# Expert weights loaded as 16 KiB of one expert or as 8 KiB of each of two

## The chip, the core and the metric

The kernel runs on one core of a Trainium2 chip. It is one launch for one sequence of 256 tokens of width 1024, all in float32. The metric is the time of one execution on the device in microseconds (us). Each time below is a median of three runs or comes from one profiled execution.

## What is computed

The reference is one encoder block: three token mixers (gated linear attention, a Fourier mixer, attention into memory tokens), a gated merge, a LayerNorm, and then a sparse feed-forward layer of 32 experts, of which each token takes four. The change touches the experts alone:

```python
logits = (hf @ w_router + b_router)
top_val, top_idx = lax.top_k(logits, 4)
top_w = softmax(top_val)
# for each expert e, on the rows xb of the tokens that chose it:
gu = xb @ w_gu[e] + b_gu[e]            # w_gu[e]: [1024, 2048]
gate, up = split(gu, 2)
gate = minimum(gate, 7.0); up = clip(up, -7.0, 7.0)
act = (up + 1.0) * (gate * sigmoid(1.702 * gate))
out = act @ w_down[e] + b_down[e]      # w_down[e]: [1024, 1024]
# y[token] += weight * out, over the token's four experts; then a last LayerNorm
```

An expert has 8 MiB of gate and up weights and 4 MiB of down weights, so that all 32 have 402.7 MB.

## The kernel before

**Stages.** The mixer comes first and fills about the first quarter of the time. The function `moe` follows. The experts are taken in 16 pairs. A token's row lies in one of 64 slots of its expert, and the two experts of a pair share the tensor engine's array: expert 0 has columns 0 to 63 of it, expert 1 columns 64 to 127, and their results are the two halves of the partitions of one PSUM tile. `pair_mm` (L969) issues a matmul for expert 0 and then one for expert 1; each has 128 rows of contraction, 64 columns of tokens as its weights and 512 columns of expert weights that stream through. A float32 matmul shows as two instructions in the trace.

**A pair's work.** `up(p)` (L975) takes eight row blocks k, each 128 rows of the contraction; for each it calls `pair_mm` for four PSUM tiles (`gps`, n = 0 to 3), which makes 8 matmuls or 16 instructions for one k. `swiglu` follows on the vector and scalar engines. `gather(p + 1)` (L899) picks the next pair's token rows with 16 one-hot matmuls (`pick`, L822, 32 instructions). `weigh` (L916, with transposes at L923) and `transpose_act` (L993, L998) prepare the next products. `down(p - 1)` (L1002) takes eight row blocks again, with two PSUM tiles (`yps`): 32 matmuls or 64 instructions. `combine` (L1018, L1021) adds the pair's result to the tokens' sums. `add_bias` (L960, L966) starts every PSUM tile with the biases. The last pair's down product is `last_down` (L1034): its columns come in three parts, and each of its loads holds one expert only.

**Loads.** A pair takes 12 loads of 2 MiB: eight by `load_gu` (L765, issued at L771) and four by `load_down` (L775, issued at L778). Every load fills one slot of a ring of ten (`new_unit`, L758), 16 KiB in each partition. `load_gu` loads one row block k of both experts: 8 KiB of a row of expert 0 and 8 KiB of a row of expert 1. `load_down` loads two row blocks of both experts: 8 KiB (two rows of 4 KiB) of each. The first six loads of pair 0 stand in slots that the mixer no longer needs (`early_load`, L1219); two more of the first loads use room that is needed later (L928). All of them are issued by SyncE's queue, and a load waits there until the matmuls that read its slot before it are done.

**Order.** Within an engine the instructions run in the order of the program, and that order is fixed when the kernel is built. A planner makes it: it walks through the traced instructions with its own estimates of their times, and whenever an engine is free it takes, of the instructions that it believes ready, the one that stands first in the source. So an instruction that it believes to be waiting for a load is passed over, and later work takes its place. Only the issues of the loads (L771) and a few matmuls that keep the array busy (`spin`, L873) are held to the order of the source.

Of the kernel before, what the change touches and what calls it, by code (L numbers as in the profile page):

```python
# [18 lines left out]
D = 1024  # L19
# [34 lines left out]
class Rstd:  # L54
    """(v + eps) ** -0.5 with one Newton step, in two parts; v is [128, n]."""
# [26 lines left out]
def ln_stats(K, x):  # L82
    """Mean and variance of the rows of x: [128, D] SBUF."""
    nc, sm = K.nc, K.small
    st = sm.tile([128, 2, 6], F32, name="bst", tag="st")
    for j in range(2):
        nc.vector.bn_stats(st[:, j], x[:, j * 512:(j + 1) * 512])
    mv = sm.tile([128, 2], F32, name="bmv", tag="mv")
    nc.vector.bn_aggr(mv, st)
    return mv  # L90


def ln_apply(K, x, mv, r, g, b, out, cut=D):
    """Columns from cut on by the scalar engine and gpsimd, the rest by the vector engine."""
    nc = K.nc
    if cut < D:
        c = slice(cut, D)
        t = K.small.tile([128, 8], F32, name="nmr", tag="sm")[:, 0:1]
        nc.vector.scalar_tensor_tensor(t, mv[:, 0:1], -1.0, r, ALU.mult, ALU.mult)
        nc.scalar.activation(out[:, c], x[:, c], AF.Identity, bias=t, scale=r)  # L100
        nc.gpsimd.tensor_tensor(out[:, c], out[:, c], g[:, c], ALU.mult)
        nc.gpsimd.tensor_tensor(out[:, c], out[:, c], b[:, c], ALU.add)
    if cut:
        c = slice(0, cut)
        nc.vector.scalar_tensor_tensor(out[:, c], x[:, c], mv[:, 0:1], g[:, c], ALU.subtract, ALU.mult)
        nc.vector.scalar_tensor_tensor(out[:, c], out[:, c], r, b[:, c], ALU.mult, ALU.add)


def layer_norm(K, x, g, b, out):
    """x: [128, D] SBUF; out = (x - mean) * rstd * g + b."""  # L110
    mv = ln_stats(K, x)
    ln_apply(K, x, mv, rstd(K, mv[:, 1:2], LN_EPS, 1), g, b, out, 768)


def split(K, src, hi, lo):
    """hi = src rounded to the multiplier's width, lo = the exact rest."""
    K.nc.scalar.activation(hi, src, AF.Copy)  # L117
    K.nc.vector.tensor_tensor(lo, src, hi.bitcast(F32), ALU.subtract)  # L118


class Split:
    """[128, n, S] operand kept as two float32r parts, in tiles of four rows."""
# [8 lines left out]
def transpose_split(K, x, tau, T, j):  # L131
    """x: [128 tokens, 1024]; writes the transpose of half j into T's columns of token tile tau."""
    nc = K.nc
    ps = K.ps.tile([128, 4, 128], F32, name="tps", tag="ms")
    for c in range(4):
        nc.tensor.transpose(ps[:, c], x[:, (j * 4 + c) * 128:(j * 4 + c + 1) * 128], K.ident)
    sl = slice(tau * 128, tau * 128 + 128)
    split(K, ps, T.hi[j][:, :, sl], T.lo[j][:, :, sl])
# [10 lines left out]
def load_w(K, W, c0, n, kn, eng=None):  # L149
    """Columns c0..c0+n of a [kn * 128, ...] matrix."""  # L150
    w = K.wraw.tile([128, 2048], F32, name="wraw", tag="wraw")[:, :kn * n].rearrange("p (k n) -> p k n", k=kn)
    (eng or K.nc.sync).dma_start(w, W[:, c0:c0 + n].rearrange("(k p) n -> p k n", p=128))
    return w


def split_w(K, w):
    """Parts of a [128, m, n] piece of weights, m * n <= 1024."""
    m, n = w.shape[1:]
    parts = []
    for name in ("whi", "wlo"):  # L160
        t = K.wspl.tile([128, 1024], F32R, name=name, tag=name)[:, :m * n]
        parts.append(t.rearrange("p (m n) -> p m n", m=m))
    split(K, w, *parts)
    return parts


class Background:
    """Work for the vector engines, woven between the projections' chunks."""
# [29 lines left out]
def mixer(ctx: ExitStack, K, A):  # L198
    tc, nc = K.tc, K.nc
    pool = lambda name, bufs: ctx.enter_context(tc.tile_pool(name=name, bufs=bufs))  # L200
    # in the order in which the ring's slots follow below
# [25 lines left out]
    # ---- inputs, LayerNorm and transposes  # L227
# [20 lines left out]
    # four tiles in one, of what is done with when the GLA branch is gated  # L248
    part = K.early.tile([128, 4, D], F32, name="parts", tag="ring2")

    # four more, up to the two small branches' operands, and four up to a gate
# [14 lines left out]
    with tc.manual_schedule(engines={mybir.EngineType.DVE, mybir.EngineType.PE, mybir.EngineType.Activation}):  # L266
        # brings the array's clock up
# [33 lines left out]
    # four tiles in one: the two directions' queries and keys, before them what makes the decays  # L301
# [7 lines left out]
    def project_T(W, c0, nch, X, kn, evac, first=None):  # L309
        """Transposed products: evac(first chunk, psum [128, m, S]) for pairs of 128 columns."""  # L310
# [14 lines left out]
    def project_tok(W, c0, X, evac, last=False, eng=None):  # L325
        """512 columns by token: evac(tau, psum [128, 512])."""
# [26 lines left out]
    # ---- low-rank decay inputs  # L353
# [9 lines left out]
    # ---- memory tokens: LayerNorm and transposes  # L363
# [27 lines left out]
    # ---- decays: log-sigmoid (times 16) and its running sums  # L391
# [31 lines left out]
    # ---- q, k (transposed), v (by token)  # L423
# [11 lines left out]
    # Inside a tile of 128 tokens the decays are taken from its middle; between the two tiles from the border.  # L435
# [34 lines left out]
    # ---- values  # L470
# [19 lines left out]
    # ---- memory keys and queries  # L490
# [14 lines left out]
    # ---- attention weights into the memory tokens  # L505
# [34 lines left out]
    # ---- memory values, FNet inputs  # L540
# [6 lines left out]
    # ---- the branches' inner products  # L547
# [59 lines left out]
    def fnet_gen():  # L607
# [5 lines left out]
        # column 128 - k of the cosines is column k, of the sines minus column k: half of each is enough  # L613
# [11 lines left out]
        # row S - s of the cosines is row s, of the sines minus row s: half of each is enough  # L625
# [27 lines left out]
    # ---- output gate of the GLA branch  # L653
# [33 lines left out]
    # ---- gates, branch projections, merge  # L687
# [44 lines left out]
    # ---- output projection, residual, LayerNorm  # L732
# [25 lines left out]
def new_unit(K, shape):  # L758
    """The next ring slot, 16 KiB a partition."""
# [5 lines left out]
def load_gu(K, A, p, k, w=None):  # L765
    """One row a partition of a pair's gate and up weights."""
    if (p, k) in K.loaded:
        return K.loaded[p, k]
    w = K.loaded[p, k] = w or new_unit(K, (2, 2 * D))
    src = A["w_gu"][0, 2 * p:2 * p + 2, k // 2 * 256:k // 2 * 256 + 256].rearrange("e (p k) n -> p e k n", p=128)  # L770
    K.tc.keep_in_program_order(K.nc.sync.dma_start(w, src[:, :, k % 2]))  # L771
    return w


def load_down(K, A, p, i):  # L775
    """Two rows a partition of a pair's down weights."""
    w = new_unit(K, (2, 2, D))
    K.nc.sync.dma_start(w, A["w_down"][0, 2 * p:2 * p + 2, i // 2 * 512:i // 2 * 512 + 512].rearrange(  # L778
        "e (p k) n -> p e k n", p=128)[:, :, i % 2 * 2:i % 2 * 2 + 2])
    return w  # L780
# [11 lines left out]
def moe(ctx, K, A):  # L792
    tc, nc = K.tc, K.nc
    h1 = K.h1
    # the slots in the order in which the mixer's pools lay, numbered by when those are done with
# [10 lines left out]
    # ---- router: logits, top 4, slot of each token in its experts  # L806
# [11 lines left out]
    def pick(p, tau, P, t, j, last, first):  # L818
        """Adds a token tile's chosen rows, transposed, to half j of the pair's operand."""
# [42 lines left out]
    def place(tau):  # L862
        """slot + 1 where the expert is chosen, 0 elsewhere."""
# [9 lines left out]
    def spin(n, out=None):  # L873
        """Keeps the array's clock up while it waits."""
# [24 lines left out]
    def gather(p):  # L899
        """The pair's rows, transposed, by a one-hot product."""  # L900
# [15 lines left out]
    def weigh(p, P):  # L916
        """The way back: slots to tokens, times the tokens' weights."""
# [9 lines left out]
    # as much of the weights as there is room for, also where the activations and the sums will be  # L927
# [10 lines left out]
    # ---- softmax weights of the chosen experts, the largest count, the residual  # L938
# [21 lines left out]
    def add_bias(acc, p, at, first):  # L960
        """acc[n] (+)= the pair's biases, by rows of the table picked with a one-hot operand."""
# [7 lines left out]
    def pair_mm(acc, xT, k, w, first, last):  # L969
        """Both experts of a pair at once, each in its half of the array's columns."""  # L970
        for e in range(2):
            nc.tensor.matmul(acc[e * 64:e * 64 + 64], xT[:, k, e * 64:e * 64 + 64], w[:, e], start=first, stop=last,  # L972
                             skip_group_check=True)

    def up(p, xT):  # L975
# [4 lines left out]
        for k in range(8):  # L980
            w = load_gu(K, A, p, k)
            for n in range(4):
                pair_mm(g[n], xT, k, w[:, :, n * 512:n * 512 + 512], not early and k == 0, early and k == 7)
# [18 lines left out]
    def down(p, aT, G):  # L1002
# [3 lines left out]
        for i in range(4):  # L1006
            w = load_down(K, A, p, i)
            for k in range(2):
                for n in range(2):
                    pair_mm(yy[n], aT, i * 2 + k, w[:, :, k, n * 512:n * 512 + 512], False, i * 2 + k == 7)  # L1010
            if p == NE // 2 - 2 and i < 3:
                spin(2, mps()[:, :128])
# [14 lines left out]
    def last_parts(p):  # L1027
        """The last pair's columns, in ever smaller parts, so that little is left to do when the last of them arrives."""
# [5 lines left out]
    def last_down(p, aT, G, parts):  # L1034
# [3 lines left out]
        for sl, ps, ks in parts:  # L1038
            for k0, k1 in zip(ks, ks[1:]):
# [3 lines left out]
                for k in range(k0, k1):  # L1043
                    pair_mm(ps, aT, k, w[:, :, k - k0], False, k == 7)
# [7 lines left out]
    def norm_rows(gb):  # L1052
        """The last LayerNorm's gain and offset on every partition."""
# [30 lines left out]
def overflow(ctx, K, A):  # L1084
    """Slots 64..255 of every expert."""
# [93 lines left out]
def finish(K, A, o, st, g, b):  # L1179
    """The last LayerNorm of z, with the statistics of its quarters, into the output."""  # L1180
# [15 lines left out]
def block(tc, A):  # L1196
# [4 lines left out]
    with tc.tile_pool(name="cst", bufs=1) as c, tc.tile_pool(name="small", bufs=8) as sm, \  # L1201
# [17 lines left out]
        def early_load(e):  # L1219
            """The first pair's row e, where the mixer no longer needs the room."""  # L1220
# [46 lines left out]
```

## Time and profile before

| | us |
|---|---|
| median of 3 runs (1262.57 to 1264.88) | 1263.12 |
| the profiled execution, first to last instruction (span) | 1260.8 |
| matmuls on the tensor engine (PE), busy | 1228.3 |
| vector engine (DVE), busy | 374.8 |
| scalar engine (ACT), busy | 249.2 |

The profiled execution's span is 2.3 us below the median of the runs, which also contains what lies around the first and the last instruction. In the rows further down, PE is the tensor engine's matmul unit, PEld its weight load, SPq SyncE's queue; L972 is line 972 of the kernel. A row of the timeline joins neighbouring instructions of one kind on one engine; x16 means 16 of them. The times of matmuls in it are modelled at their ends, so that two neighbouring rows overlap by some tenths of a microsecond.

### The profile page before, as it was taken

The numbers are of one execution on the slowest core, as the hardware profiler recorded it, in microseconds if no ns is written. First come the engines' busy times: TensorE is split into PE (matmuls) and PEld (weight loads), VectorE is DVE, ScalarE is ACT, GpSimd is POOL, SyncE is SP. The second block draws the span as 40 slices with busy tenths as digits, with TensorE's granted clock in tenths as the row PEclk, the third lists the DMA queues.
The fourth block names the chain that finished last, engine by engine and source line by source line (L and its number), as shares of the span: only waits on it lengthen the run. The fifth ranks groups of instructions, "written<-read, shape, count | busy, mean of one in ns | idle before, by whom it ended". The sixth has DMA issues, their size and how long they took to land.

```text
span 1260.8 us, 15216 instructions
## 1 busy us (share of the span) xinstructions
PE 1228.3 (97%) x6601; PEld 652.0 (52%) x6601; DVE 374.8 (30%) x572; ACT 249.2 (20%) x404; POOL 60.1 (5%) x76
## 2 busy tenths in 40 slices
PE   7899999999999999999999999999999999999995
PEld 6799999999644344343333434343434334343332
DVE  6996555486311020201111111111121111111023
ACT  4655555453211010101010000101010101000010
POOL 3460000000000000000000000000000000000000
PEclk8899999999999999999999999899999999999998
DMA  8665557597899999999999999999999999999990
GB/s 285 203 213 169 201 201 234 216 336 285 354 393 409 424 427 427 427 428 428 427 427 427 427 427 427 427 427 427 427 428 428 428 427 426 428 428 427 428 359 36
DMA packets 105707, 459.31 MB, mean 364 GB/s; under 512 B 4614, under 2 KB 51264, under 8 KB 57508
## 3 DMA queue, kind: packets, MB, share of 16 engines
q1 hardware_dynamic: 105224, 457.66, 89.2%
q8 instruction: 54, 0.88, 0.3%
q10 hardware_dynamic: 284, 0.55, 0.1%
q14 instruction: 17, 0.14, 0.0%
q0 software_dynamic: 128, 0.07, 0.0%
HBM read 457.22 MB, written 1.05 MB: 363 GB/s over the span
## 4 chain that ended last, share of the span: by engine, by line
PE 88%; DVE 7%; ACT 2%; issue 1%; DMA 1%; POOL 0%; ACTq 0%; DVEq 0%; POOLq 0%
PE gps L972 34%; PE yps L972 18%; PE pj L145 6%; PE pj L146 6%; PE pj L144 6%; PE mps L822 5%; PE mps L1021 5%; PE gps L966 2%; PE mps L998 2%; PE yps L966 1%; DVE work L786 1%; DVE wlo L118 1%; DVE work L784 1%; DVE work L787 1%; DVE work L788 1%
## 5 line engine op out<-in xcount | busy, mean ns | idle before, releaser
L972 PE MATMUL gps<-wexp,xT 128*64 128x512 f32 x2048 | 448.5, 594 | 0.0
L972 PEld LDWEIGHTS gps<-wexp,xT 128*64 128x64 f32 x2048 | 143.5, 137 | 291.7 <-issue 289.8
L972 PE MATMUL yps<-wexp,work 128*64 128x512 f32 x960 | 233.7, 611 | 0.0
L972 PEld LDWEIGHTS yps<-wexp,work 128*64 128x64 f32 x960 | 69.9, 139 | 147.1 <-issue 145.3
L118 DVE TENSOR_TENSOR wlo<-wraw,whi 128x1024 fp32r<-128x1024 f32 (+2 forms) x97 | 118.4, 1228 | 63.7 <-ACT whi L117 63.5
L1025 DVE TENSOR_TENSOR sum<-sum,mps 128x512 f32<-128x512 f32 (+1 forms) x62 | 41.6, 670 | 267.3 <-PE mps L1021 267.3
L784 DVE TENSOR_SCALAR work<-gps 128x512 f32<-128x512 f32 x32 | 22.1, 692 | 320.9 <-PE gps L972 292.2
L117 ACT ACTIVATE whi<-wraw 128x1024 fp32r<-128x1024 f32 (+2 forms) x97 | 94.8, 984 | 97.2 <-PE pj L145 82.5
L144 PE MATMUL pj<-hT,whi 128*128 128x256 f32 (+1 forms) x392 | 112.6, 287 | 0.0
L146 PE MATMUL pj<-hT,wlo 128*128 128x256 f32 (+1 forms) x392 | 110.9, 283 | 0.5 <-DVE wlo L118 0.5
L145 PE MATMUL pj<-hT,whi 128*128 128x256 f32 (+1 forms) x392 | 110.9, 283 | 0.1
L785 ACT ACTIVATE work<-work 128x512 f32<-128x512 f32 x32 | 20.1, 629 | 377.4 <-DVE work L784 377.4
L822 PEld LDWEIGHTS mps<-P,h 128*128 128x128 f32 x512 | 62.5, 196 | 22.4 <-issue 21.0
L144 PEld LDWEIGHTS pj<-hT,whi 128*128 128x128 f32 (+1 forms) x392 | 73.6, 188 | 1.0 <-ACT whi L117 0.3
L146 PEld LDWEIGHTS pj<-hT,wlo 128*128 128x128 f32 (+1 forms) x392 | 73.5, 187 | 1.1 <-DVE wlo L118 0.9
L145 PEld LDWEIGHTS pj<-hT,whi 128*128 128x128 f32 (+1 forms) x392 | 73.5, 187 | 0.9 <-DVE hT L118 0.6
L822 PE MATMUL mps<-P,h 128*128 128x128 f32 x512 | 68.0, 287 | 0.4 <-DVE P L815 0.4
L1021 PE MATMUL mps<-work,G 128*128 128x512 f32 (+1 forms) x132 | 63.3, 602 | 1.1 <-ACT work L1045 0.8
L1014 ACT ACTIVATE work<-yps 128x512 f32<-128x512 f32 x30 | 17.9, 597 | 200.4 <-PE yps L972 200.4
L913 ACT ACTIVATE xT<-mps 128x512 f32<-128x512 f32 x32 | 19.1, 596 | 186.3 <-PE mps L822 186.3
L966 PE MATMUL gps<-ebias,sel 32*128 32x512 f32 (+1 forms) x134 | 51.7, 633 | 0.0
L963 POOL COPY sel<-kp 128x128 f32<-128x128 f32 x32 | 9.6, 301 | 805.5 <-PE gps L966 443.8
(252 smaller groups left out, 1076.8 us busy)
## 6 DMA issues: line engine op xcount, KB each, us to landing
wexp<-in_w_gu_dram SPq DMA_DIRECT2D x128, 2048.0 KB, 19.1
wexp<-in_w_down_dram SPq DMA_DIRECT2D x60, 2048.0 KB, 21.6
wraw<-in_w_in_dram SPq DMA_DIRECT2D x28, 1024.0 KB, 5.2
wexp<-in_w_down_dram SPq DMA_DIRECT2D x6, 1024.0 KB, 24.8
wraw<-in_w_mem_kv_dram SPq DMA_DIRECT2D x4, 1024.0 KB, 5.3
wraw<-in_w_br_gla_dram SPq DMA_DIRECT2D x4, 1024.0 KB, 6.8
wraw<-in_w_out_dram SPq DMA_DIRECT2D x4, 1024.0 KB, 5.1
wraw<-in_w_br_fnet_dram SPq DMA_DIRECT2D x2, 1024.0 KB
```

What stands on the lines that cost most here:

```text
L117: K.nc.scalar.activation(hi, src, AF.Copy)
L118: K.nc.vector.tensor_tensor(lo, src, hi.bitcast(F32), ALU.subtract)
L144: nc.tensor.matmul(out, wh, xh, start=first, stop=False)
L145: nc.tensor.matmul(out, wh, xl, start=False, stop=False)
L146: nc.tensor.matmul(out, wl, xh, start=False, stop=last)
L784: nc.vector.tensor_scalar(g, gate, 7.0, None, ALU.min)
L822: nc.tensor.matmul(t[:, c], h1[tau][:, f0 + c % 2:f0 + 256:2], P[:, tau].rearrange("p e s -> p (e s)"), start=first and c == 0, stop=last, ...
L966: nc.tensor.matmul(ac, t[r].rearrange("k e s -> k (e s)"), bias[r, c0:c0 + ac.shape[-1]], start=first, stop=not first, skip_group_check=True)
L972: nc.tensor.matmul(acc[e * 64:e * 64 + 64], xT[:, k, e * 64:e * 64 + 64], w[:, e], start=first, stop=last, skip_group_check=True)
L998: nc.tensor.transpose(t[:, c], a[:, j * 4 + c::8] if last else a[:, j * 512 + c:j * 512 + 512:4], K.ident)
L1021: nc.tensor.matmul(c, G[:, tau * 128:tau * 128 + 128], y[:, sl], start=True, stop=True)
L1025: nc.vector.tensor_tensor(z[tau][:, sl], z[tau][:, sl], c, ALU.add)
```

## The change

A load of gate and up weights takes two neighbouring row blocks of one expert (16 KiB of adjacent memory for a partition) in place of one row block of both. A load of down weights takes four row blocks of one expert in place of two of both. The count, the size and the queue of the loads stay as they are. `pair_mm` gets the two experts' weights from two tiles in place of one. `up` asks for two loads before every second row block, `down` for two loads before every fourth; the `spin` matmuls of pair 14 stay behind the same row blocks. The rest of the diff removes comments.

```diff
-def load_gu(K, A, p, k, w=None):
-    if (p, k) in K.loaded:
-        return K.loaded[p, k]
-    w = K.loaded[p, k] = w or new_unit(K, (2, 2 * D))
-    src = A["w_gu"][0, 2 * p:2 * p + 2, k // 2 * 256:k // 2 * 256 + 256].rearrange("e (p k) n -> p e k n", p=128)
-    K.tc.keep_in_program_order(K.nc.sync.dma_start(w, src[:, :, k % 2]))
+def load_gu(K, A, p, i, w=None):
+    if (p, i) in K.loaded:
+        return K.loaded[p, i]
+    w = K.loaded[p, i] = w or new_unit(K, (2, 2 * D))
+    src = A["w_gu"][0, 2 * p + i % 2, i // 2 * 256:i // 2 * 256 + 256].rearrange("(p k) n -> p k n", p=128)
+    K.tc.keep_in_program_order(K.nc.sync.dma_start(w, src))
     return w

 def load_down(K, A, p, i):
-    w = new_unit(K, (2, 2, D))
-    K.nc.sync.dma_start(w, A["w_down"][0, 2 * p:2 * p + 2, i // 2 * 512:i // 2 * 512 + 512].rearrange(
-        "e (p k) n -> p e k n", p=128)[:, :, i % 2 * 2:i % 2 * 2 + 2])
+    w = new_unit(K, (4, D))
+    K.nc.sync.dma_start(w, A["w_down"][0, 2 * p + i % 2, i // 2 * 512:i // 2 * 512 + 512].rearrange(
+        "(p k) n -> p k n", p=128))
     return w

     def pair_mm(acc, xT, k, w, first, last):
         for e in range(2):
-            nc.tensor.matmul(acc[e * 64:e * 64 + 64], xT[:, k, e * 64:e * 64 + 64], w[:, e], start=first, stop=last,
+            nc.tensor.matmul(acc[e * 64:e * 64 + 64], xT[:, k, e * 64:e * 64 + 64], w[e], start=first, stop=last,
                              skip_group_check=True)

         for k in range(8):                                                # in up
-            w = load_gu(K, A, p, k)
+            if k % 2 == 0:
+                ws = [load_gu(K, A, p, k + e) for e in range(2)]
             for n in range(4):
-                pair_mm(g[n], xT, k, w[:, :, n * 512:n * 512 + 512], not early and k == 0, early and k == 7)
+                pair_mm(g[n], xT, k, [w[:, k % 2, n * 512:n * 512 + 512] for w in ws], not early and k == 0,
+                        early and k == 7)

-        for i in range(4):                                                # in down
-            w = load_down(K, A, p, i)
-            for k in range(2):
+        for i in range(2):
+            ws = [load_down(K, A, p, i * 2 + e) for e in range(2)]
+            for k in range(4):
                 for n in range(2):
-                    pair_mm(yy[n], aT, i * 2 + k, w[:, :, k, n * 512:n * 512 + 512], False, i * 2 + k == 7)
-            if p == NE // 2 - 2 and i < 3:
-                spin(2, mps()[:, :128])
+                    pair_mm(yy[n], aT, i * 4 + k, [w[:, k, n * 512:n * 512 + 512] for w in ws], False, i * 4 + k == 7)
+                if p == NE // 2 - 2 and i * 4 + k in (1, 3, 5):
+                    spin(2, mps()[:, :128])
```

## Rows read from the trace of the kernel before

**Rows 1.** The page: busy time by engine, and the chain that ended last.

```profile
PE 1228.3 (97%) x6601; PEld 652.0 (52%) x6601; DVE 374.8 (30%) x572; ACT 249.2 (20%) x404; POOL 60.1 (5%) x76
PE 88%; DVE 7%; ACT 2%; issue 1%; DMA 1%; POOL 0%; ACTq 0%; DVEq 0%; POOLq 0%
```

**Rows 2.** Instructions on the expert weights: loads (first, last start), idle time before their readers.

```profile
L771 SPq DMA_DIRECT2D wexp<-in_w_gu_dram x128: 367/368/1754, 130.9 to 1164.1; - x128
...
its engine sat idle before it (us, times) until:
...
  DMA wexp<-in_w_down_dram: 0.8, 1
  DMA wexp<-in_w_gu_dram: 0.3, 1
```

**Rows 3.** Windows: pair 2, pair 5; us, busy (x), granted clock, DMA share, GB/s.

```profile
421.00:475.00 54.00, 53.99 (x259) 20.96 (x258) 8.83 (x15) 4.89 (x9) 0.59 (x2) 1.00 1.01 426
591.15:648.48 57.33, 57.15 (x255) 21.54 (x254) 8.92 (x15) 5.00 (x9) 0.59 (x2) 1.00 1.01 427
```

**Rows 4.** Timeline of PE, pair 2 (start us, us, instruction xcount), up to pair 3.

```profile
448.56 4.04 PE L822 MATMUL mps<-P,h 128*128 128x128 f32 x32
456.01 13.95 PE L972 MATMUL yps<-wexp,work 128*64 128x512 f32 x64
474.85 10.52 PE L972 MATMUL gps<-wexp,xT 128*64 128x512 f32 x48
485.30 2.62 PE L822 MATMUL mps<-P,h 128*128 128x128 f32 x20
...
494.32 13.96 PE L972 MATMUL gps<-wexp,xT 128*64 128x512 f32 x64
```

**Rows 5.** Timeline of PE, pair 5 up to the next pair's first row block.

```profile
591.15 3.65 PE L972 MATMUL gps<-wexp,xT 128*64 128x512 f32 x16
594.74 2.62 PE L822 MATMUL mps<-P,h 128*128 128x128 f32 x20
...
600.87 1.68 PE L822 MATMUL mps<-P,h 128*128 128x128 f32 x12
603.76 20.82 PE L972 MATMUL gps<-wexp,xT 128*64 128x512 f32 x96
627.84 1.93 PE L972 MATMUL yps<-wexp,work 128*64 128x512 f32 x6
629.70 0.75 PE L998 MATMUL mps<-kp,work 128*128 128x128 f32 x4
630.38 2.79 PE L972 MATMUL yps<-wexp,work 128*64 128x512 f32 x10
634.15 10.52 PE L972 MATMUL yps<-wexp,work 128*64 128x512 f32 x48
```

**Rows 6.** Timeline of PE, the last pair's down product.

```profile
1228.77 7.51 PE L972 MATMUL gps<-wexp,work 128*64 128x512 f32 x34
1236.61 1.98 PE L1021 MATMUL mps<-work,G 128*128 128x512 f32 x4 [0.33 <-ACT work L1045]
```

**Rows 7.** The load of pair 15's row block 6: its issue, us to its landing.

```profile
L771 SPq DMA_DIRECT2D wexp<-in_w_gu_dram x1: 367/367/367, 1159.5 to 1159.5; - x1
DMA to landing us min/median/max: 24.6/24.6/24.6
```

**Rows 8.** Timeline of PE, pair 15's row blocks 1 to 7.

```profile
1179.78 24.25 PE L972 MATMUL gps<-wexp,xT 128*64 128x512 f32 x112
```

**Rows 9.** DMA packets of 600 to 670 us, and the main queue's share of 16 engines.

```profile
DMA packets 3875, 29.89 MB, mean 427 GB/s; under 512 B 229, under 2 KB 229, under 8 KB 229
q1 hardware_dynamic: 3872, 29.84, 100.8%
```

**Rows 10.** A drop of the granted clock in pair 3: its window, and the matmuls in it.

```profile
511.00:515.00 4.00, 4.00 (x8) 0.76 (x6) 1.39 (x2) 0.61 (x2) 0.00 (x0) 0.57 1.02 430
511.54 3.57 PE L972 MATMUL yps<-wexp,work 128*64 128x512 f32 x6
```

More of the change, by code (lines that the diff above doesn't have):

```diff
@@ L1043, in last_down @@
                 for k in range(k0, k1):
-                    pair_mm(ps, aT, k, w[:, :, k - k0], False, k == 7)
+                    pair_mm(ps, aT, k, [w[:, e, k - k0] for e in range(2)], False, k == 7)
             nc.scalar.activation(y[:, sl], ps, AF.Copy)
```

## Prediction

> **What bounds the kernel now.** I read the page first: the busy times, then the chain that ended last. PE's matmuls fill 97% of the span, and PE is 88% of the chain, DMA 1% [rows 1]. So the question is whether PE ever waits for the weights that the change loads in another way. The groups by line, with what ended the idle time before them, answer it: before all readers of the weights, loads ended 0.8 and 0.3 us of idle time, once each [rows 2]. [...]
>
> The loads come next, because they are busy too: the main queue fills 100.8% of 16 engines at 427 GB/s [rows 9]. A load of 2.097 MB takes 2.097/427 = 4.91 us at that rate and the twelve of a pair 58.9 us, 1.6 us more than PE's 57.33. The early pairs' stock of loaded slots pays for this, and at the end some is left: the load of pair 15's row block 6 is issued at 1159.5 and has landed 24.6 us later, at 1184.1 [rows 7]; its matmuls come after five row blocks of 16 instructions, 24.25/7 = 3.46 us each, from 1179.78, so at 1197.1 [rows 8]. It is 13.0 us early. Two bounds lie close together, but PE's is the one that counts.
>
> Last I read PE's timeline, because it shows what the order of the matmuls costs. Rows of x16, x48, x64 and x96 take 3.65, 10.52, 13.95 and 20.82 us [rows 4, 5]: that is 0.21 + 0.859 us times 4, 12, 16 and 24. I call 0.859 us a slot: two matmuls (four instructions) of the two experts, side by side in their halves of the array. x6 is three matmuls and takes 1.93 us, two slots; x10 is five and takes 2.79 us, three slots [rows 5]. **A matmul without a neighbour in the other half costs the whole slot.** This is the price on which my forecast rests.
>
> Where does the order come from? From the planner's estimates. In pair 2 all of `gather`'s 32 `pick` instructions stand in one row outside the products; from pair 3 on they stand between row blocks of gate and up products [rows 4, 5], in lots of x20 (2.62 us) and x12 (1.68 us). The planner passes over an instruction only if it believes it not ready, and PE on the chip did not wait there. So I read: from pair 3 on the planner expects the loads later than they come, and fills a believed wait with picks. It does the same to half a pair of matmuls: x6 and x10 end on a lone matmul, and in the last pair's down product, where a load holds one expert, x34 is eight pairs and one lone matmul of the next part, before `combine` at L1021 [rows 6]. PE then waits 0.33 us there with more row blocks of the same expert in that load: matmuls into one PSUM tile keep the order of the source, in which expert 1's product of this row block is next.
>
> **The change part by part.**
>
> *Loads.* 128 + 60 loads of the same size stand in the same queue, so issues and ring are unchanged. Packets of 16 KiB could raise the rate, or not. 3875 packets in 70 us on 16 engines, 229 of them tiny, make 16 × 70 × 1.008 / 3646 = 0.310 us for 8 KiB [rows 9]. Whatever a larger packet saves, its bound here is 0: PE doesn't wait [rows 2, 3]. [...] The rows have no second packet size to test it; hidden behind PE, it changes nothing.
>
> *Slots of the ring.* Expert 0's slot of a couple of row blocks is now read until the second of them, so both slots come free up to one row block (3.46 us) later, and expert 1's load is wanted one row block earlier than its place in the queue was before. Together 6.9 us, against 13.0 us of slack [rows 7, 8]: 0 us, and slack grows if PE gets slower. If that cover were gone, PE would follow the loads, at 58.9 us a pair.
>
> *Order in up.* Now one load brings two row blocks of expert 0, the next those of expert 1. Where the planner believes PE starved, expert 0's load lands first in its eyes, so its four matmuls of the first row block (n = 0 to 3) are issued alone. The next row block of expert 0 can't follow, since each of its PSUM tiles waits for expert 1's product. Then expert 1's load lands: four matmuls alone, then the second row block in pairs. Of these 16 matmuls, 0 0 0 0 1 1 1 1 0 1 0 1 0 1 0 1, neighbours of different halves share a slot, which leaves 11 slots in place of 8; with filler between the two lots 12; one slot less where a couple follows directly on another. Four couples: 11 + 12 + 10 + 10 = 43 in place of 32, **+11 slots**. The ends are 0 (no split) and +16 (all broken by filler); I take 11 because there are only two lots of picks per pair [rows 5].
>
> *Order in down.* A couple has four row blocks and two PSUM tiles, so the first lots are two matmuls each: 0 0 1 1 0 1 and so on in pairs. All but the first and the last find a neighbour: 9 slots in place of 8, 18 for the two couples. Today's x6 and x10 already lose one of 16 [rows 5]. From 17 to 18 slots: **+1**; ends −1 (no split) and +4 (fillers in every joint).
>
> *Sum.* Picks stand among the row blocks from pair 3, so the split holds for up in pairs 3 to 15 and down in 3 to 14: 13 × 11 + 12 × 1 = 155 slots × 0.859 = 133 us. A pair goes from 57.33 to about 67.6 us. The profiled execution has 1260.8 us of span, so 1394; the median stands 2.3 above the span, **1396 us**.
>
> [...]
>
> *The rest.* `spin` stays behind the same row blocks; `last_down` and L1043 are only written differently; pairs 0 to 2 have their loads early: 0 us.
>
> **Bounds of the sum.** Less: the first couple of each pair may find both loads there (−3 slots × 13 = −33 us); starving may begin two pairs later (−20 us): 1343. More: all couples broken (+5 × 13 × 0.859 = +56 us); matmuls one after another in one half may cost 3% more than a slot, as L1021's (1.98 − 0.21)/4 = 0.443 us against 0.429 for half a slot [rows 6], which is +1 us per pair; a clock dip costs 3.57 − 1.93 = 1.64 us [rows 10]. Not all of it at once: 1460.
>
> **The rivals.**
>
> (a) *The order stays in pairs.* The planner keeps row blocks together because both loads look present, or issues both halves at once. For it: in pair 2 the order is whole [rows 4]. Against it: x34 and the picks. Then down loses its split: one slot and two breaks of 0.21, 1.3 us × 13 = −17 us by PE; but 6.9 us of the 13.0 us slack go to the later slots, and what PE gains beyond the other 6 it waits for loads. About 1257, from 1247 to 1264. The deciding point is whether `yps` is one row of x64.
>
> (b) *No order within a PSUM tile.* All eight matmuls of an expert's load go alone: 16 slots a couple in place of 8, less joints, some +28 slots in up and +14 in down per pair, 42 × 0.859 × 13 = +470 us, 1730. Against it stands the 0.33 us wait [rows 6].
>
> (c) *Half an array lowers the clock.* The order is as I forecast, but long stretches of one half let the granted clock fall; a dip to 0.57 took 1.64 us [rows 10], which is why four to six per pair (one for a couple) would add 6 to 10 us to each: 1480 to 1530. The few lone matmuls now don't show it.
>
> (d) *Larger packets bring time.* That needs a PE that waits for loads; 1.1 us in all did [rows 2]. At most that: 1262.
>
> **How the numbers follow.** The main case 0.84, (a) 0.10, (b) 0.02, (c) 0.03, (d) 0.01. The likeliest time is 1396. From 1340 to 1460 the range holds nearly all of the main case, some 0.81. About 0.2% is what a measurement of this kernel can tell from no change, so faster means below 1260.6: 0.06, from (a). Same: 0.05, the rest of (a) and (d). Slower: 0.89.
>
> **What would show it.** Right: from pair 3 on `gps` rows of x8 that last 3.65 us (four lone slots) in place of 1.93; a pair's period near 67 us; 25.2 MB in that time, so the rate down to some 372 GB/s, with half the packets, of 16 KiB; PE still about 97% busy and no waits for loads; pairs 0 to 2 unchanged at about 54 us. Wrong: periods of 57 us or less with rows of x16 or more, PE waiting for `wexp`, or lone lots that take half a slot each.

## The result: slower by 6%, and the profile after

The changed kernel takes 1341.29 us (median of 4 runs, 1337.93 to 1343.22), the kernel before 1262.84 beside it: a ratio of 1.0619, interval 1.0601 to 1.0638. The forecast was 1396 us in a range of 1340 to 1460. The direction and the place are as forecast; the size of the loss is 78 us where the forecast said 133.

The page of the changed kernel, busy time by engine and the chain that ended last, against [rows 1]:

```profile
PE 1308.7 (98%) x6601; PEld 697.6 (52%) x6601; DVE 374.7 (28%) x572; ACT 250.5 (19%) x404; POOL 60.0 (4%) x76
...
PE 89%; DVE 7%; ACT 2%; issue 1%; DMA 1%; POOL 0%; ACTq 0%; DVEq 0%; POOLq 0%
```

PE is busy for 80.4 us more with the same 6601 instructions, and the span has grown by 80.1. The loss is a tensor engine that needs longer for the same work, not one that waits: the table of PE's waits has no row for `wexp`. The windows of two pairs, from their first `gps` row to that of the next pair (us, then busy time and count for PE, PEld, DVE, ACT and POOL, granted clock, DMA share, GB/s), say it again beside [rows 3]:

```profile
420.14:474.09 53.95, 53.94 (x259) 21.59 (x255) 8.84 (x15) 4.90 (x9) 0.59 (x2) 1.00 1.01 430
537.41:601.05 63.64, 63.46 (x256) 25.09 (x255) 8.92 (x15) 5.12 (x9) 0.59 (x2) 1.00 0.97 399
```

The early pairs are as they were. From pair 3 on an undisturbed pair takes 63.64 us in place of 57.33, at the same granted clock of 1.00, and now the DMA engines have some time to spare: a share of 0.97 and 399 GB/s. PE frees the slots later: SyncE's queue waits 405.4 us in all at L771 for `gps` matmuls, where in the kernel before it waited 313.8.

PE's timeline of the second of them (start us, us, instruction, xcount; in brackets the wait before it), to be laid beside [rows 5]:

```profile
537.41 7.09 PE L972 MATMUL gps<-wexp,xT 128*64 128x512 f32 x32
544.44 0.97 PE L822 MATMUL mps<-P,h 128*128 128x128 f32 x6
545.34 3.65 PE L972 MATMUL gps<-wexp,xT 128*64 128x512 f32 x8
548.92 3.33 PE L822 MATMUL mps<-P,h 128*128 128x128 f32 x26
552.18 7.08 PE L972 MATMUL gps<-wexp,xT 128*64 128x512 f32 x24
...
560.62 15.83 PE L972 MATMUL gps<-wexp,xT 128*64 128x512 f32 x64
...
579.70 1.93 PE L972 MATMUL yps<-wexp,work 128*64 128x512 f32 x4
581.56 0.75 PE L1000 MATMUL mps<-kp,work 128*128 128x128 f32 x4
...
583.29 13.95 PE L972 MATMUL yps<-wexp,work 128*64 128x512 f32 x60
```

The row of x8 has eight instructions and lasts as long as a row of x16 did: four matmuls of expert 0 alone. The row of x64 takes 15.83 us where 64 instructions took 13.95 [rows 4]. The sum for `gps` is 7.09 + 3.65 + 7.08 + 15.83 = 33.65 us; before it was 3.65 + 3.65 + 20.82 = 28.12 [rows 5]: +5.53. For `yps` it is 1.93 + 13.95 = 15.88 in place of 1.93 + 2.79 + 10.52 = 15.24: +0.64. Together 6.17 of the 6.31 us. (Clock drops as in [rows 10], 1.6 us each, come in four pairs of the changed kernel and in three of the kernel before, and in pair 8 of both. From pair 3's first row to pair 15's the twelve pairs take 775.05 us in place of 699.92, 6.3 more on average, which leaves little for them.)

The order of the two halves doesn't show in the trace. It stands in the instruction stream of the built kernel; 0 is a matmul of expert 0, 1 one of expert 1, "|" filler work between:

```
before  gps 01010101 | 01010101 | 0101...01 (48 matmuls)
        yps 010 | 10101 | 0101...01 (24)
after   gps 0011010101010101 | 0000 | 111101010101 | 0000111101010101 0000111101010101
        yps 00 | 1101010101010100 11010101010101
```

So the planner does what the prediction said, in three of the four couples: it issues expert 0's lot of four alone when expert 0's load is in, and expert 1's when the other is. The first couple is hardly split: 0011, then pairs.

### The profile page after: what moved, and what is told of

It reads as the page before. It is cut to its first block, busy times and chain, and to the rows that moved or that the text cites. A ratio compares the mean times of both kernels' runs of the same rounds, so it can differ in the third digit from the quotient of the medians.

```text
span 1340.9 us, 15216 instructions
## 1 busy us (share of the span) xinstructions
PE 1308.7 (98%) x6601; PEld 697.6 (52%) x6601; DVE 374.7 (28%) x572; ACT 250.5 (19%) x404; POOL 60.0 (4%) x76
## 4 chain that ended last, share of the span: by engine, by line
PE 89%; DVE 7%; ACT 2%; issue 1%; DMA 1%; POOL 0%; ACTq 0%; DVEq 0%; POOLq 0%
PE gps L972 37%; PE yps L972 18%; PE pj L145 6%; PE pj L146 6%; PE pj L144 6%; PE mps L822 5%; PE mps L1023 5%; PE gps L966 2%; PE mps L1000 2%; PE yps L966 1%; DVE work L786 1%; DVE wlo L118 1%; DVE work L784 1%; DVE work L787 1%; DVE work L788 1%
## 5 line engine op out<-in xcount | busy, mean ns | idle before, releaser
L972 PE MATMUL gps<-wexp,xT 128*64 128x512 f32 x2048 | 518.5, 595 | 0.0
L972 PEld LDWEIGHTS gps<-wexp,xT 128*64 128x64 f32 x2048 | 176.1, 136 | 320.6 <-issue 317.7
L972 PE MATMUL yps<-wexp,work 128*64 128x512 f32 x960 | 243.2, 607 | 0.0
L972 PEld LDWEIGHTS yps<-wexp,work 128*64 128x64 f32 x960 | 82.9, 138 | 150.4 <-issue 149.6
L118 DVE TENSOR_TENSOR wlo<-wraw,whi 128x1024 fp32r<-128x1024 f32 (+2 forms) x97 | 118.3, 1228 | 63.8 <-ACT whi L117 63.6
L919 DVE TENSOR_TENSOR wr<-P,wts 128x256 f32<-128x256 f32 x16 | 6.8, 424 | 258.3 <-PE mps L923 258.2
```

## The experiments

**Theories.** (T) The loss is the order of the halves alone, and the loads themselves cost nothing. (R1) The loads cost: slots that come free later, or a second expert that lands too late. (R2) Within T: what does a lot cost? The prediction let only neighbouring matmuls of different halves share a slot. By that rule the order above has 9 + 4 + 8 + 21 = 42 `gps` slots, while the durations give 38.2. The rows suggest another way of counting, an estimate of mine: the matmuls are taken in order, and those of the other half begin as soon as no more than **four instructions** (two matmuls) of a lot are unfinished. This window of the changed kernel's x64 row fits it (L972 only: us, PE, PEld, clock, DMA share, GB/s):

```profile
560.40:562.10 1.70, 1.49 (x4) 0.60 (x5) 1.00 0.85 328
562.10:563.80 1.70, 1.70 (x10) 0.65 (x8) 1.00 1.01 434
```

In the first 1.7 us four instructions start, one after another; by the order above they are expert 0's. From the fifth on two start at a time, so by that order expert 1's first stands beside expert 0's fifth of eight. By the neighbour rule it would stand beside the seventh.

### The same loads, the other expert first

```diff
-        for e in range(2):
+        for e in (1, 0):
             nc.tensor.matmul(acc[e * 64:e * 64 + 64], ...
```

> The changed kernel, but pair_mm issues expert 1's matmul first and expert 0's second. Expert 1's load is the later of the two, and expert 0's matmul follows expert 1's in each PSUM tile, so the planner has no lone lot to issue early. If the order of the matmuls makes the time (my theory), the split is gone: yps is one row of x64 in 13.95 us, gps has rows of x32 and x96, a pair takes about 56 us of PE, less than the loads' 58.9, so the gain ends where the stock of slack is used up: 1250 to 1258 us in all. If the 16 KiB loads cost time by themselves (slots that come free later, a second expert that lands too late), the time stays near 1341, or PE waits for wexp and it lies between 1270 and 1341.

Measured: 1260.39 us, ratio 0.9990 (0.9977 to 1.0003). With the changed kernel's own loads the loss of 78 us is gone. The timeline of one pair:

```profile
738.56 0.72 PE L1000 MATMUL mps<-kp,work 128*128 128x128 f32 x4 [0.17 <-DVE work L788]
739.21 1.13 PE L966 MATMUL gps<-ebias,sel 32*128 32x512 f32 x4
741.48 0.72 PE L1000 MATMUL mps<-kp,work 128*128 128x128 f32 x4 [1.15 <-DVE work L788]
742.13 15.65 PE L972 MATMUL yps<-wexp,work 128*64 128x512 f32 x64
...
761.60 7.09 PE L972 MATMUL gps<-wexp,xT 128*64 128x512 f32 x32
768.61 4.04 PE L822 MATMUL mps<-P,h 128*128 128x128 f32 x32
...
773.85 20.82 PE L972 MATMUL gps<-wexp,xT 128*64 128x512 f32 x96
```

No lone lot is left, and a pair without disturbance takes 55.98 us. R1 falls: the table of PE's waits has no load in it here either. The time misses the 1250 to 1258 that were expected, though. Down no longer stands as filler while the vector engine makes the activations, so PE waits 1.15 us at L1000, and `yps` x64 then takes 15.65 us where it takes 13.95 [rows 4]. The windows (columns as in the result) show the granted clock falling behind that wait:

```profile
736.00:741.50 5.50, 4.18 (x19) 1.61 (x15) 4.51 (x7) 1.12 (x2) 0.29 (x1) 1.00 1.01 432
741.50:745.50 4.00, 4.00 (x14) 1.63 (x16) 0.00 (x0) 0.60 (x1) 0.00 (x0) 0.62 1.02 434
```

Of the pairs 3 to 14 eight took 57.4 to 57.7 us and two 55.98; the other two, 66.86 and 53.62, hold other matmuls (L1061) and some of each other's picks. The wait of 1.15 us stands in all twelve, but in pairs 4, 9 and 13 `yps` x64 takes 13.95 us behind it: the wait doesn't bring a drop each time.

### The kernel before with the other expert first

The same edit of `pair_mm`, with the loads of the kernel before.

> The kernel before (8 KiB of each expert) with the same reversed order of the two experts. A load holds both, so the reversal gives the planner no other arrivals; yps loses its lone matmul (16 slots in place of 17). By my theory -0.86 us in each of 13 pairs: 1252 to 1255. A rival, that the reversal itself is what helps and not the loads' order of arrival, would make it as fast as the changed kernel with the reversal or faster, by more than 11 us below 1263. No change at all: 1263, if the lone matmul cost nothing or the loads bind already.

Measured: 1255.25 us, ratio 0.9948 (0.9930 to 0.9966). `yps` loses its lone matmul, as two rows of two slots in one pair show:

```profile
743.77 1.94 PE L972 MATMUL yps<-wexp,work 128*64 128x512 f32 x8
746.32 1.94 PE L972 MATMUL yps<-wexp,work 128*64 128x512 f32 x8
```

The kernel gains about 7 us, which is one slot in each of twelve pairs less two more clock drops than the kernel before has (five pairs of 58.1 to 58.2 us among ones of 56.48). So the reversal by itself is worth 7 us; with the changed loads it is worth 81, and the rest is the undoing of the split. The rival's gain of more than 11 us didn't come; that this kernel is still 5 us faster than the first experiment's is taken up further down.

### The loads as the only bound

```diff
-            for n in range(4):                                # in up
+            for n in (range(4) if p == 0 else (0, 2)):
-                for n in range(2):                            # in down
+                for n in range(1):
```

Both runs keep all loads, the first those of 8 KiB, the second those of 16 KiB. What is compared is the time of a pair's 12 loads.

> The kernel before without the columns n = 1, 3 of the gate and up products (from pair 1 on) and n = 1 of the down products: half of PE's work on the weights is left out, all loads stay. PE needs under 40 us a pair, so the loads set the pace: 12 loads of 4.91 us, 58.9 us a pair at 427 GB/s, if the rate of the kernel before was the most that these loads reach; under 57 us if PE's pace held them back.

> The changed kernel with the same half of the products left out, all loads kept. [...] If the couples' longer hold on the slots costs, they take more. My theory: within 0.5 us of each other.

Measured, in one run each: 1244.76 us with 8 KiB and 1245.28 with 16 KiB. Windows of 500 to 1150 us, and the DMA packets in them, first 8 KiB, then 16 KiB:

```profile
500.00:1150.00 650.00, 514.86 (x1749) 174.73 (x1748) 98.83 (x162) 56.23 (x103) 10.41 (x23) 0.83 1.01 428
DMA packets 36023, 277.90 MB, mean 428 GB/s; under 512 B 2114, under 2 KB 2114, under 8 KB 2114
```

```profile
500.00:1150.00 650.00, 542.93 (x1766) 194.95 (x1762) 98.23 (x161) 56.68 (x104) 8.77 (x23) 0.89 1.01 431
DMA packets 19226, 279.99 MB, mean 431 GB/s; under 512 B 2135, under 2 KB 2135, under 8 KB 2135
```

With the queue full all the time, 279.99 MB move in place of 277.90: larger packets were 0.75% faster, 0.44 us of a pair's 58.9. The gain doesn't show in the whole times here. While loaded slots are still put in stock, the run with 16 KiB moved less in one slice of its page, 287 GB/s in place of 336 from 311 to 342 us, and from 330 to 500 us the changed kernel moved 405 where the kernel before moved 409. That fits slots which are held longer; no run separates it. The 8 KiB run's 428 GB/s, where PE waits 152 us for loads in all, also says that PE didn't hold down the 427 of the kernel before. So the two runs give the floor that the loads set: with half of the products left out, the time is still 1245 us.

### Either half of the change alone

In the first, `load_gu` and `up` are those of the changed kernel and these lines stay as they were; in the second it is the other way round.

```diff
 def load_down(K, A, p, i):                                # gate and up alone
-    w = new_unit(K, (4, D))
+    w = new_unit(K, (2, 2, D))
...
 def load_gu(K, A, p, k, w=None):                          # down alone
-    src = A["w_gu"][0, 2 * p + i % 2, i // 2 * 256:i // 2 * 256 + 256].rearrange("(p k) n -> p k n", p=128)
+    src = A["w_gu"][0, 2 * p:2 * p + 2, k // 2 * 256:k // 2 * 256 + 256].rearrange("e (p k) n -> p e k n", p=128)
```

> Gate and up loads of one expert each (changed), down loads of both experts (as before). What the trace of the changed kernel suggests: a half of the array keeps up to four instructions started or waiting, and the issue in order runs ahead so far; a lot of four alone then costs 2 slots once in a stretch without filler, not 3 at each joint. gps in three stretches (a lot of 4 alone, 12, 48 matmuls) then has 4 + 8 + 26 = 38 slots in place of 32, +6 a pair: 6 x 0.859 x 13 = 67 us, 1330. By the counting of my prediction (neighbours alone share a slot) the same order has 4 + 8 + 31 = 43: +123 us, 1386. If it is the down loads that cost, about 1270.

> Down loads of one expert each (changed), gate and up loads of both (as before). yps 2 + 16 = 18 slots in place of 17, 0.64 to 0.86 us in each of 12 pairs, and one more break by filler in gps (0.2 us): 1271 to 1276. Both countings say the same here. If the down loads carry the loss: about 1330.

Measured: 1327.80 us, ratio 1.0524 (1.0496 to 1.0552), and 1272.80 us, ratio 1.0086 (1.0059 to 1.0113). Against the kernel before beside them (1261.77) that is +66.0 and +11.0 us; their sum of 77 is the loss of 78 within the spread of the runs. The down products of the second run, one pair, have the rows of the changed kernel:

```profile
627.16 1.93 PE L972 MATMUL yps<-wexp,work 128*64 128x512 f32 x4
630.75 13.95 PE L972 MATMUL yps<-wexp,work 128*64 128x512 f32 x60
```

The gate and up products of the first run, one pair:

```profile
600.86 3.65 PE L972 MATMUL gps<-wexp,xT 128*64 128x512 f32 x8
604.44 2.62 PE L822 MATMUL mps<-P,h 128*128 128x128 f32 x20
606.99 7.08 PE L972 MATMUL gps<-wexp,xT 128*64 128x512 f32 x24
614.00 1.68 PE L822 MATMUL mps<-P,h 128*128 128x128 f32 x12
...
616.89 22.81 PE L972 MATMUL gps<-wexp,xT 128*64 128x512 f32 x96
```

The x96 row holds three couples of the form 0000 1111 01010101 and takes 22.81 us in place of 20.82 [rows 5]: (22.81 − 0.21)/0.859 = 26.3 slots, not 24 and not 31.

### The order alone, with the loads of the kernel before

```diff
-            for n in range(4):                                # in up; lots of four
-                pair_mm(g[n], xT, k, ...)
+            for e in range(2):
+                for n in range(4):
+                    nc.tensor.matmul(g[n][e * 64:e * 64 + 64], xT[:, k, e * 64:e * 64 + 64],
+                                     w[:, e, n * 512:n * 512 + 512], ...)
```

In the lots of two n runs over 0 and 1, then over 2 and 3, for each expert in turn. In the lots of eight, with the gate and up loads of one expert each, e runs outside of two row blocks.

> Loads as in the kernel before; up issues each row block in lots of two matmuls, 0 0 1 1 0 0 1 1. A lot of two is four instructions: if a half takes four started or waiting, the issue runs on to the other half at once, and nothing is lost: 1263, up to 3 more for the down products' other split. If it took three, half a slot in each stretch, three stretches a pair: +17 us, 1280. If neighbours alone share a slot, one slot in each: +33 us, 1297.

> Loads as in the kernel before, but up issues each row block as four matmuls of expert 0 and then four of expert 1. No load differs, so all that changes is the order. With four instructions in each half: a row block alone 6 slots in place of 4, six row blocks in one stretch 26 in place of 24, so +6 slots a pair from pair 3 on and +2 in the first three: 1335. If neighbours alone share a slot: 7, 7 and 37 in place of 4, 4 and 24, +19 a pair: about 1515. If the order of the halves costs nothing and the loss of the changed kernel comes from its loads: 1263.

> Gate and up loads of one expert each (changed), down as before; for two row blocks all eight matmuls of expert 0 come first and then all eight of expert 1, so a lot is 16 instructions. With four instructions in each half, a couple alone takes 14 slots in place of 8, three in one stretch 38 in place of 24, four 50 in place of 32, and yps loses one: 13 x 21 + 3 x 18 = 327 slots, +281 us, about 1544. If neighbours alone share: 15, 43 and 57 slots, 426 more, +366 us, about 1629. If the issue ran eight instructions ahead: 12, 28, 36: 13 x 9 + 3 x 4 = 129 slots, 1374.

Measured: 1266.23 us (ratio 1.0025, 1.0011 to 1.0039), 1335.12 us (1.0562, 1.0533 to 1.0591) and 1539.91 us (1.2187, 1.2163 to 1.2210). A row of lots of two, a row block of four, and a couple of eight, each with filler on both sides:

```profile
591.72 3.70 PE L983 MATMUL gps<-wexp,xT 128*64 128x512 f32 x16
```

```profile
612.67 5.42 PE L984 MATMUL gps<-wexp,xT 128*64 128x512 f32 x16
```

```profile
749.21 12.29 PE L987 MATMUL gps<-wexp,xT 128*64 128x512 f32 x32
```

The lots of four settle T from the other side: no load differs from the kernel before, and the order alone makes it slower by 73 us. The three sizes settle R2. In slots:

| row | order | neighbours alone | four instructions ahead | (duration − 0.21)/0.859 |
|---|---|---|---|---|
| two, x16 | 00110011 | 5 | 4 | 4.1 |
| four, x16 | 00001111 | 7 | 6 | 6.1 |
| eight, x32 | 0 ×8, 1 ×8 | 15 | 14 | 14.1 |
| changed, x32 | 0011 010101010101 | 9 | 8 | 8.0 |
| changed, x24 | 1111 01010101 | 8 | 8 | 8.0 |
| changed, x64 | (0000 1111 01010101) twice | 21 | 18 | 18.2 |
| gate and up alone, x96 | the same, three times | 31 | 26 | 26.3 |

Counted in the same way, three instructions ahead would make 4.5, 6.5 and 14.5 slots of the first three rows, and five would make 4, 5.5 and 13.5. The whole times were forecast with the rule of four before the runs, as 1263 to 1266, 1335 and 1544; the neighbour rule gave 1297, 1515 and 1629.

### Towards a faster kernel

Gate and up loads of one expert each, down loads of both (as before), expert 1 first; and the first experiment's kernel with idle matmuls in the place of its wait:

```diff
+            if j and 2 < p < NE // 2 - 1:                     # in transpose_act
+                spin(4, t[:, 0])
```

> Gate and up loads of one expert each (changed), down loads of both (as before), and expert 1's matmul first in pair_mm. No lone lots; unlike in e1_second_first the down loads stand ready as filler (yps of x8, x12) behind the gate and up products, so the wait of 1.15 us for the vector engine (L1000) and the clock drop of 1.7 us behind it should go. The gate and up loads move at the 430 GB/s of e1 in place of 427. PE needs 55.5 to 56.5 us a pair, the loads 58.5, so the end of the loads sets it: 1248 to 1254. If 16 KiB loads are worth nothing once the order is the same, it equals e2_before_second_first: 1255.

> e1_second_first with four idle matmuls (1.4 us) beside the transposes L1000 in pairs 3 to 14, where that run's PE waits 1.15 us for the vector engine and its clock then falls in most pairs (yps x64 15.65 in place of 13.95 us). They use up the wait and cost 0.3 us more. If the wait brings the clock down, the pairs that took 57.6 us take about 56.2, and with 12 pairs the time comes to 1250 to 1254. If the drops have another cause, they stay, and the time is 1261 to 1265.

Measured: 1253.01 us, ratio 0.9921 (0.9907 to 0.9935), and 1254.60 us, ratio 0.9943 (0.9929 to 0.9956). Both beat the two kernels of this study, by under 1%; the second ends 0.6 us above its range. 1253, 1254.60 and the 1255 of the kernel before with the reversed order weren't measured side by side and lie too close to rank them. In the run with idle matmuls the wait and the clock drop behind it are gone; the same place of the same pair as above:

```profile
735.20 1.13 PE L966 MATMUL gps<-ebias,sel 32*128 32x512 f32 x4
736.46 0.75 PE L1002 MATMUL mps<-kp,work 128*128 128x128 f32 x4
737.14 13.95 PE L972 MATMUL yps<-wexp,work 128*64 128x512 f32 x64
```

Nine of its twelve pairs 3 to 14 took 55.66 to 55.98 us, and only pair 8, with L1063's matmuls in front of `yps`, still has a drop there. So that the first experiment came out above its range was the wait and what the clock did behind it. At the end both meet the other bound, the second with 5.4 us of waits for gate and up loads, the first with 20.5: in the run with down loads of both experts a pair takes 54.55 us as long as loaded slots are in stock, and later PE waits for loads.

```profile
PE gps L972 <- DMA wexp<-in_w_gu_dram: 20.5, 11, 2.7
...
1166.19 7.09 PE L972 MATMUL gps<-wexp,xT 128*64 128x512 f32 x32 [0.76 <-DMA wexp<-in_w_gu_dram]
1175.87 7.09 PE L972 MATMUL gps<-wexp,xT 128*64 128x512 f32 x32 [2.59 <-DMA wexp<-in_w_gu_dram]
```

The first row is its table of waits (us in total, times, longest), the others are pair 15's row blocks.

## Why the prediction was right, and where its size was off

- **PE is the bound, transfers are hidden.** Right. After the change loads ended 0.3 us of idle time before the readers of the weights, once, and loads that are 0.75% faster brought nothing, so rival (d) falls too.
- **The planner splits from pair 3 on.** Right. It splits gate and up in pairs 3 to 15, not in 0 to 2, and the run with expert 1 first shows the cause: the same loads with nothing that can be issued at the first arrival have no split.
- **The price of a lone matmul, one slot.** Right where filler stands around it: x8 takes 3.65 us, x4 of `yps` 1.93.
- **+11 slots in up.** This is the step that failed. The count of the order came out right, partly by luck: 42 slots by the neighbour rule on the real order against the 43 foretold, but the first couple has 9 in place of 11 and the last two 21 in place of 20. The rule was wrong: "neighbours of different halves share a slot" holds for x6 and x10, from which I took it, and isn't all for lots of four. Counted with four instructions ahead, which is within 0.3 slots of every row in the table, a lot of four loses two slots once in a stretch and nothing at later joints. Measured: 38.2 − 32 = +6.2 slots, 5.53 us in place of 9.45. Over 13 pairs that is 51 of the 55 us between forecast and result.
- **+1 slot in down.** Right in count (2 + 16 slots against 17) and 0.64 us in place of 0.86, since the row's fixed 0.21 us falls away once.
- **The lower bounds.** They covered the miss for another reason than the one given, and by luck: 1341.29 is 1.3 us inside the range, and two of the four runs are below 1340. I had allowed for a first couple that isn't split, which nearly happened (2 of the 3 slots), and for starving that begins later, which did not. No bound allowed for a counting that reaches further ahead. x6 and x10 end after three and five matmuls and can't tell a reach of one matmul from one of two, so the rule should have had a second value: +6 and +1 slots a pair, 90 × 0.859 = 77 us, about 1340, which belonged inside the range and not at its end. The signs went the same way: rows of x8 of 3.65 us came, but with a pair's period of 63.6 us and 399 GB/s in place of 67 and 372.
- **The rivals.** (a), order in pairs, didn't occur; built by hand, it gives 1260 or, without the wait, 1255, about the 1257 that I had put on it. (b), a whole load of an expert in one lot, didn't occur either. The run with lots of eight builds its gate and up part: (b)'s 28 slots a pair there would be +313 us, about 1576, and the run took 1540. (c) didn't occur: in the x64 row with its lone stretches the clock stayed at 1.00:

```profile
560.40:576.40 16.00, 16.00 (x67) 5.83 (x65) 1.95 (x5) 0.63 (x1) 0.30 (x1) 1.00 0.98 399
```

- **Sharing the array.** Two matmuls of one half in front of the other half's were hidden (3.70 us for a row of x16), four were not (5.42 us).

Not tried: what the planner takes a load's time to be, and whether a planner with the 4.9 us that a load takes at the measured 427 GB/s would have kept the pairs.

## What to carry to other kernels

When a change alters which of an instruction's operands arrives together with which, ask what the scheduler will issue at the first arrival, and not only how fast the bytes come. With a scheduler like this one, two matmuls that share the array should have operands that arrive together, or the one whose operand comes last should stand first in the source: that one swap was worth 81 us here. And price a gap in sharing with rows of more than one length, because short rows can fit several ways of counting, as x6 and x10 did here.

## What the runs showed of the hardware

- Lots of two, four and eight cost 0, 2 and 6 slots of 0.859 us in a row between fillers (3.70, 5.42 and 12.29 us). Counting four instructions (two matmuls) ahead in a half fits the seven rows of the table to 0.3 slots. This counting is the author's estimate from durations and starts; no row shows what PE holds waiting.
- Behind a wait of 1.15 us on PE the granted clock was 0.62 for 4 us in the pair shown, and the products there took 1.7 us longer. Of the eleven pairs 3 to 14 without L1061's matmuls eight had such a drop and three, with the same wait, had none; in the kernel before, whose wait there is 0.17 us, three of eleven had one. With idle matmuls in the wait none of the eleven had it (13.95 or 14.06 us, in one pair two rows of 7.09), and the kernel was 6 us faster. So in these traces, one of each kernel, drops are more frequent with the wait, and the wait isn't all of their cause.
- In pair 8 of the first experiment PE was busy without a gap with L1061's matmuls, on two rows of the array each, from 799.8 to 805.6 us; `yps` x64 behind them took 16.47 us in place of 13.95.
- With the queue full and half of the products left out, loads of 16 KiB a row moved at 431 GB/s and loads of 8 KiB at 428.
